# Weight tiles of a float32 decoder block: lower parts by an accumulating DMA, weights three tiles ahead, operands at multiples of 512 bytes

## The chip, the cores and the metric

The kernel runs on one core of a Trainium2 chip, in one launch. The metric is the device time of that launch in microseconds (us); lower is better. The time before is the median of three runs.

## The reference

One decoder block on 512 tokens of width 1024, in float32. Two token mixers work in parallel on x:

```
proj = x @ w_in                       # 1024 x 7168: c_val c_gate q f i g gates
A: c = c_val * sigmoid(c_gate); causal depthwise conv (31); LayerNorm; silu;  y_conv = c @ w_conv_out
B: 8 heads of a gated linear recurrence, head size 128, chunkwise; RMSNorm; * silu(g); y_hgrn = o @ w_hgrn_out
mix = (sigmoid(gate_A)*y_conv + sigmoid(gate_B)*y_hgrn) @ w_out
x = LayerNorm(alpha*x + mix)
u, gv = split(x @ w_ffn_in)           # 1024 x 5632
x = LayerNorm(alpha*x + (gelu(dwconv3(u)) * gv) @ w_ffn_out)     # 2816 x 1024
```

## The kernel before, in words

**Products.** Every large product is made in float32 accuracy from operands in the type fp32r. An operand is a pair (hi, lo): hi is the value rounded to fp32r and lo = value - hi. `mm3` (L152) issues three matmuls, hi*hi, hi*lo and lo*hi, on L154, L155 and L156, into one sum. The first of a group's operands is the one loaded into the array (stationary, 128 columns), the second is streamed (moving, 512 columns, or 256 in the seven-product stages).

**Weight stream.** The weights lie in DRAM as 142 tiles of 128x1024 float32 (512 KB), in the order of their use. `weight(i)` (L139) calls `fetch` for every tile up to i + AHEAD, with AHEAD = 2. `fetch` (L113) loads the raw tile from SyncE's queue (L119; three raw buffers), ScalarE copies it to hi (L135), and VectorE subtracts, lo = raw - hi (L136). hi and lo have rings of four buffers each; eight tiles go to other storage (`resident`). The first eight tiles, of the convolution's input projection, begin the kernel. 88 tiles go through `fetch`; the other 54 are the gates' 16 and 38 of the FFN's, which `weight_sums` (L560) loads, combines and splits for a scheme of seven products of half-size blocks in the place of eight (`seven`, L591); these use the same rings (`ring_pair`, L549).

**Order of the work.** Convolution inputs (tiles 0 to 7, until about 51 us), values and eight heads (`values`, `head`; tiles 8 to 39, until about 289 us), in which the steps of the recurrence are put in between the matmuls of the next projection (`pump`, L268) and the taps of the depthwise convolution run on VectorE in the background (L251); convolution output and half of the recurrence's output (40 to 47); gates in the seven-product scheme (48 to 63, 343 to 420 us); the other half of the output (64 to 67); W_out (68 to 75), for two halves of the tokens; FFN up, three pairs of blocks plain (76 to 81) and 19 by seven products (82 to 119, until 714 us); FFN down (120 to 141). Each engine runs its own instructions in order; the order is laid down when the kernel is built, by program order and readiness, and `urgent` (L543) raises a priority. GpSimd has a part of the recurrence's updates (L352, L393, L426) and one DMA (L947).

**Addresses.** A partition's memory is filled in this order: 16,384 bytes reserved for descriptors of GpSimd's DMAs, four constants of 32 bytes, the pool of constants (2,240 bytes), the weight pool, the pool of temporaries (among them many tiles of under 512 bytes), and the pool of activations. So the weight pool begins at 18,752 = 36*512 + 320 and the activations at 107,712 = 210*512 + 192; the temporaries used as operands begin at 64, 192 or 448 past a multiple of 512. All slices that a matmul takes are multiples of 512 bytes long or apart. Of the 1968 three-part matmuls of 512 columns, stationary and moving operand begin a multiple of 256 bytes apart in 472, and 128 bytes off that in 1496; of the 2556 of 256 columns in 572 and 1984 (counted from the addresses of the kernel before).

Of the kernel before, what the change touches and what calls it, by code (L numbers as in the profile page):

```python
# [35 lines left out]
# columns of the packed per-channel parameters  # L36
# [12 lines left out]
# weight stream: tile numbers  # L49
# [5 lines left out]
GATES = (4, 0, 5, 1, 6, 2, 7, 3)  # the order of the gates' pairs of blocks  # L55
# [9 lines left out]
def hybrid_block(ctx: ExitStack, tc: tile.TileContext, wts: bass.AP, xT_d: bass.AP,  # L65
# [27 lines left out]
    AHEAD = 2  # L93
# [7 lines left out]
    # the activation table and the tensor engine's clock are up before the first data  # L101
    wrm = tmp.tile([P, 512], BF16, tag="mv", name="wrm", bufs=1)
    wrs = const.tile([P, 8], F32, name="wrs")
    ve.memset(wrm, 0.0)
    ve.memset(wrs, 0.0)
    ac.activation(wrs, wrs, AF.Exp)
# [6 lines left out]
    def fetch(i):  # L113
        raw = wp.tile([P, 1024], F32, tag="raw", name=f"wr{i}", bufs=3)
        parts = 4 if i == 0 else 1
        n = 1024 // parts
        pieces = [slice(j * n, j * n + n) for j in range(parts)]
        for c in pieces:
            nc.sync.dma_start(raw[:, c], wts[i][:, c])  # L119
        if i in resident:  # L120
            hi, lo = resident[i]()
        else:
            hi = wp.tile([P, 1024], F32R, tag="hi", name=f"wh{i}", bufs=4)
            lo = wp.tile([P, 1024], F32R, tag="lo", name=f"wl{i}", bufs=4)
        if isinstance(hi, list):
            for j in range(2):
                c = slice(j * 512, j * 512 + 512)
                ac.copy(hi[j], raw[:, c])
                ve.tensor_tensor(lo[j], raw[:, c], hi[j], ALU.subtract)
        else:  # L130
            for c in pieces:
                if parts > 1:
                    ve.tensor_copy(hi[:, c], raw[:, c])
                else:
                    ac.copy(hi[:, c], raw[:, c])  # L135
                ve.tensor_tensor(lo[:, c], raw[:, c], hi[:, c], ALU.subtract)  # L136
        loaded[i] = (hi, lo)
# [14 lines left out]
    def mm3(ps, a, b, start, stop, more=False):  # L152
        """ps += a^T b in float32 accuracy, each operand as (hi, lo); more: onto a sum already read"""
        pe.matmul(ps, a[0], b[0], start=start, stop=False, skip_group_check=more)  # L154
        pe.matmul(ps, a[0], b[1], start=False, stop=False, skip_group_check=more)  # L155
        pe.matmul(ps, a[1], b[0], start=False, stop=stop, skip_group_check=more)  # L156

    def rsqrt(dst, src, n, mult, eps, key):
        """dst = 1/sqrt(src*mult + eps) on [P, n]: a third-order step and Newton's from the guess by the exponent.
        With v = KAPPA*(src*mult + eps), the last step's -27/1024 becomes the result's scale."""  # L160
        v = tmp.tile([P, n], F32, tag=f"rs_x{n}", name=f"rsx_{key}")
        y = tmp.tile([P, n], F32, tag=f"rs_y{n}", name=f"rsy_{key}")
        t = tmp.tile([P, n], F32, tag=f"rs_t{n}", name=f"rst_{key}")
# [10 lines left out]
        q = tmp.tile([P, n], F32, tag=f"rs_q{n}", name=f"rsq_{key}")  # L174
# [13 lines left out]
    p1 = tc.tile_pool(name="p1", bufs=1)  # L188
    p1p = p1.__enter__()
# [8 lines left out]
    cws = [p1p.tile([P, 1054], F32, tag=f"sc{j}", name=f"cws{j}") for j in range(4)]  # L198
# [23 lines left out]
    # lower bounds: softmax over the two rows of logits  # L222
# [3 lines left out]
    mx = tmp.tile([P, HEADS], F32, tag="s_mx", name="mx", bufs=1)  # L226
    e0 = tmp.tile([P, HEADS], F32, tag="s_e0", name="e0", bufs=1)
    e1 = tmp.tile([P, HEADS], F32, tag="s_e1", name="e1", bufs=1)
# [74 lines left out]
    cst = tmp.tile([P, NT, 6], F32, tag="cst", name="cst", bufs=1)  # L303
    cmv = tmp.tile([P, NT, 2], F32, tag="cmv", name="cmv", bufs=1)
    crs = tmp.tile([P, NT], F32, tag="crs", name="crs", bufs=1)
# [31 lines left out]
    def head(h):  # L337
# [7 lines left out]
        # the factor 1-lb of k rides on q  # L345
# [14 lines left out]
        def block_scores(n, cols_of):  # L360
            """psum [s, blk, n] = kt[:, s] . moving columns of the 32-block of s"""
# [8 lines left out]
        def take(ps, c0, hh, i):  # L370
            """scores of t in the odd blocks of hh, where the mask i is set"""
# [23 lines left out]
        def next_tot(hh):  # L395
            nonlocal tot
            tv, n = pairs_of(tot, hh)
            nt = tmp.tile([P, n], F32, tag=f"tot{hh}", name=f"tt{h}_{hh}", bufs=1 if hh < 4 else 2)
            ve.tensor_tensor(nt, tv[:, :, 0], tv[:, :, 1], ALU.mult)  # L399
            tot = nt  # L400
# [9 lines left out]
        def moving(hh):  # L410
            """queries of the levels hh and 2 hh for keys that decay to the end of their block of hh:
            t in the odd blocks of hh; t in the odd blocks of 2 hh, for s in the second half of the even one; the same
            over the whole second half, for s in the first"""
# [9 lines left out]
            # what the keys of a block of 4 hh decay by to its end  # L423
            dk = tmp.tile([P, nr * 16, 3], F32, tag="dk", name=f"dk{h}_{hh}", bufs=1)
# [9 lines left out]
        def s_first():  # L434
            # the diagonal, and pairs
# [54 lines left out]
        def s_state():  # L490
            # states before the blocks 1 to 3
# [10 lines left out]
        def s_out():  # L502
# [6 lines left out]
            ms = tmp.tile([P, NT], F32, tag="ms", name=f"ms{h}")  # L509
            rs = tmp.tile([P, NT], F32, tag="rs", name=f"rs{h}")  # L510
# [30 lines left out]
    # Winograd's form of Strassen's: activations = [[A11, A12], [A21, A22]] by tokens and inputs,  # L541
    # two blocks of 128 outputs = [[B11, B12], [B21, B22]] by inputs and block.
# [6 lines left out]
    def ring_pair(key, extra):  # L549
        """hi and lo of [P, 1024]: the weight stream's slots and, if there is one, a fifth"""  # L550
        out = []
        for tag, more in zip(("hi", "lo"), extra or (None, None)):
            if more is not None and ring_n[0] % 5 == 4:
                out.append(p1p.tile([P, 1024], F32R, tag=more, name=f"s{tag}_{key}"))
            else:
                out.append(wp.tile([P, 1024], F32R, tag=tag, name=f"s{tag}_{key}", bufs=4))
# [3 lines left out]
    def weight_sums(i, t, b21, extra):  # L560
        """the seven weight operands of the stream's tiles i and i+1"""
# [29 lines left out]
    def seven(ring, slots, w, A, S, pc, ug, last):  # L591
        """two blocks of outputs, features by tokens, into ug; last(X) takes the second half of the first"""
# [22 lines left out]
        # a sum is read between two additions to it; with a fifth slot the reads get more time  # L615
# [55 lines left out]
    class Two:  # L671
        """blocks of 256 tokens in two tiles, indexed [:, k]"""
# [60 lines left out]
    # the gated sums, as (hi, lo)  # L733
# [4 lines left out]
    def mixed(m, srcs):  # L738
        """blocks m and m+1"""
# [37 lines left out]
    # W_out stays on chip for both halves of the tokens  # L777
# [24 lines left out]
    def ln1_transposes(half, tb, n):  # L802
# [4 lines left out]
        # gain and shift go by partitions here  # L807
# [7 lines left out]
    def factor_sums(i, sh, sl):  # L815
        """S1..S4 of the activations for the seven-product scheme, 128 tokens of each half"""
# [41 lines left out]
    def hid():  # L858
        """the hidden activations, by blocks of 128 channels, in what is free by now"""
# [35 lines left out]
    def seven_up(j, w, sh, sl):  # L895
        """a pair of blocks of the hidden layer"""
# [62 lines left out]
    def hidden(k):  # L959
        """hidden block k as (hi, lo)"""  # L960
# [39 lines left out]
    for tb in range(NT):  # L1000
# [88 lines left out]
```

## Time and profile before

| | us |
|---|---|
| median of 3 runs | 847.4 |
| lowest and highest | 846.91, 847.9 |
| profiled execution, first to last instruction (span) | 846.1 |

The profile is of one execution; its span leaves out what the run takes before the first and after the last instruction. That execution's own time is not known beside its span, so the median less the span, 1.3 us, stands for what lies around it. Busy shares in the span: TensorE 98%, its weight loads 85%, VectorE 79%, ScalarE 49%, GpSimd 7%. In rows of the trace PE is TensorE's matmul, PEld its weight load, DVE VectorE, ACT ScalarE, POOL GpSimd, SP SyncE. The end of a matmul is modelled, so the spacing of starts says more of TensorE's rate than the duration of one. L-numbers are lines of the kernel before.

### The profile page before, as it was taken

The numbers are of one execution on the slowest core, as the hardware profiler recorded it, in microseconds if no ns is written. First come the engines' busy times: TensorE is split into PE (matmuls) and PEld (weight loads), VectorE is DVE, ScalarE is ACT, GpSimd is POOL, SyncE is SP. The second block draws the span as 40 slices with busy tenths as digits, with TensorE's granted clock in tenths as the row PEclk, the third lists the DMA queues.
The fourth block names the chain that finished last, engine by engine and source line by source line (L and its number), as shares of the span: only waits on it lengthen the run. The fifth ranks groups of instructions, "written<-read, shape, count | busy, mean of one in ns | idle before, by whom it ended". The sixth has DMA issues, their size and how long they took to land.

```text
span 846.1 us, 14434 instructions
## 1 busy us (share of the span) xinstructions
PE 829.9 (98%) x5771; PEld 720.1 (85%) x5771; DVE 666.9 (79%) x1141; ACT 411.8 (49%) x760; POOL 59.0 (7%) x93
## 2 busy tenths in 40 slices
PE   9999999999999999999999999999999999999995
PEld 6888777777777778999988899999999999888884
DVE  5379999999788849688774789699999999753366
ACT  4233443445566755466542646466666666423200
POOL 0000321233211210000000000000000000000000
PEclk9999999999999999999999999999999999999998
DMA  8323212122211224233255331122333224633202
GB/s 291 119 100 100 75 58 92 50 77 76 75 53 51 86 76 157 85 118 105 88 178 207 125 125 53 73 101 100 110 119 122 101 100 139 261 123 105 95 26 75
DMA packets 26659, 90.33 MB, mean 107 GB/s; under 512 B 2912, under 2 KB 3808, under 8 KB 26464
## 3 DMA queue, kind: packets, MB, share of 16 engines
q1 hardware_dynamic: 24288, 82.85, 29.2%
q10 hardware_dynamic: 2160, 4.47, 1.5%
q0 software_dynamic: 144, 2.10, 0.6%
q8 instruction: 45, 0.74, 0.4%
q14 instruction: 22, 0.18, 0.1%
HBM read 85.21 MB, written 4.19 MB: 106 GB/s over the span
## 4 chain that ended last, share of the span: by engine, by line
PE 79%; DVE 16%; ACT 3%; issue 1%; DMA 1%; POOL 0%; DVEq 0%; ACTq 0%; POOLq 0%
PE ps L154 25%; PE ps L156 25%; PE ps L155 25%; DVE cws L251 7%; DVE wl L136 2%; DMA xr<-in_xT 1%; DVE tt L399 1%; PE ps L366 1%; PE ps L521 1%; DVE qq L388 1%; DVE gg L355 1%; ACT wh L135 1%; ACT sq L513 0%; PE ps L506 0%; PE ps L805 0%
## 5 line engine op out<-in xcount | busy, mean ns | idle before, releaser
L136 DVE TENSOR_TENSOR wl<-wr,wh 128x1024 fp32r<-128x1024 f32 (+1 forms) x82 | 100.9, 1233 | 55.1 <-ACT wh L135 55.0
L135 ACT CAST wh<-wr 128x1024 fp32r<-128x1024 f32 x78 | 81.9, 1050 | 126.2 <-PE ps L156 68.2
L154 PE MATMUL ps<-xh,wh 128*128 128x512 f32 x256 | 105.7, 414 | 0.6 <-ACT xh L147 0.6
L155 PE MATMUL ps<-xl,wh 128*128 128x512 f32 x256 | 102.4, 400 | 0.2 <-DVE xl L150 0.2
L156 PE MATMUL ps<-xh,wl 128*128 128x512 f32 x256 | 102.0, 398 | 0.0
L251 DVE SCALAR_TENSOR_TENSOR cws<-cws,par 128x512 f32<-128x512 f32 x120 | 89.2, 772 | 0.0
L154 PE MATMUL ps<-sh,shi_t 128*128 128x256 f32 x228 | 64.3, 282 | 0.0
L156 PE MATMUL ps<-sh,slo_t 128*128 128x256 f32 x228 | 64.3, 282 | 0.0
L155 PE MATMUL ps<-sl,shi_t 128*128 128x256 f32 x228 | 64.2, 282 | 0.0
L154 PEld LDWEIGHTS ps<-xh,wh 128*128 128x128 f32 x256 | 48.6, 190 | 12.1 <-ACT xh L147 2.0
L156 PEld LDWEIGHTS ps<-xh,wl 128*128 128x128 f32 x256 | 48.5, 189 | 10.7
L155 PEld LDWEIGHTS ps<-xl,wh 128*128 128x128 f32 x256 | 48.6, 190 | 10.1 <-DVE xl L150 0.8
L150 DVE TENSOR_TENSOR slo_t<-Toh,shi_t 128x1024 fp32r<-128x1024 f32 x38 | 46.4, 1220 | 11.5 <-ACT shi_t L147 11.4
L147 ACT CAST shi_t<-Toh 128x1024 fp32r<-128x1024 f32 x38 | 39.5, 1041 | 15.9 <-PE ps L155 15.9
L156 PEld LDWEIGHTS ps<-sh,slo_t 128*128 128x128 f32 x228 | 43.1, 189 | 0.0
L154 PEld LDWEIGHTS ps<-sh,shi_t 128*128 128x128 f32 x228 | 43.1, 189 | 0.0
L155 PEld LDWEIGHTS ps<-sl,shi_t 128*128 128x128 f32 x228 | 43.1, 189 | 0.0
L150 DVE TENSOR_TENSOR slo_b<-wr,shi_b 128x1024 fp32r<-128x1024 f32 x27 | 33.0, 1221 | 8.3 <-ACT shi_b L147 8.3
L545 ACT COPY pc<-ps 128x256 f32<-128x256 f32 x57 | 21.1, 370 | 37.0 <-PE ps L156 37.0
L147 ACT CAST shi_b<-wr 128x1024 fp32r<-128x1024 f32 x27 | 28.4, 1050 | 9.2 <-PE ps L155 5.7
L947 POOL DMA_DIRECT2D lnp<-in_ln x1 | 0.7, 717 | 413.5 <-PE ps L156 413.5
L156 PE MATMUL ps<-wh,ht 128*128 128x512 f32 x72 | 28.6, 397 | 0.0
(375 smaller groups left out, 2485.6 us busy)
## 6 DMA issues: line engine op xcount, KB each, us to landing
wr<-in_wts SPq DMA_DIRECT2D x141, 512.0 KB, 3.5
xr<-in_xT ACTq DMA_DIRECT2D x8, 256.0 KB, 4.0
x<-in_x ACTq DMA_DIRECT2D x4, 512.0 KB, 7.3
x_d<-x SPq DMA_DIRECT2D x4, 512.0 KB, 3.5
x1a<-x_d SPq DMA_DIRECT2D x1, 2048.0 KB, 8.5
lnp<-in_ln POOLq DMA_DIRECT2D x1, 2048.0 KB, 11.7
out<-x1a SPq DMA_DIRECT2D x8, 256.0 KB, 2.0
xsqq<-in_xT SPq DMA_DIRECT2D x4, 256.0 KB, 2.7
```

What stands on the lines that cost most here:

```text
L135: ac.copy(hi[:, c], raw[:, c])
L136: ve.tensor_tensor(lo[:, c], raw[:, c], hi[:, c], ALU.subtract)
L147: ac.copy(hi, src)
L150: (lo_eng or ve).tensor_tensor(lo, src, hi, ALU.subtract)
L154: pe.matmul(ps, a[0], b[0], start=start, stop=False, skip_group_check=more)
L155: pe.matmul(ps, a[0], b[1], start=False, stop=False, skip_group_check=more)
L156: pe.matmul(ps, a[1], b[0], start=False, stop=stop, skip_group_check=more)
L251: ve.scalar_tensor_tensor(cacc[j], cpad[j][:, i:i + T], w, cacc[j], ALU.mult, ALU.add)
L355: ve.scalar_tensor_tensor(gg, gg, pcol(PC_NG + h), pg, ALU.mult, ALU.mult)
L366: pe.matmul(ps[32 * j:32 * j + 32, blk], kt[:, b32 * 32:b32 * 32 + 32], cols_of(b32), start=True, stop=True, tile_position=(0, 32 * j))
L388: ve.tensor_tensor(qo, qo, tv[:, :, 0:1].broadcast_to([P, n, hh]), ALU.mult)
L545: f(*args)
```

## The change

In `fetch`, tiles from 8 on: ScalarE copies raw to hi, ScalarE then writes lo = -hi, and a DMA issued by GpSimd adds raw onto lo, in place of VectorE's subtraction. AHEAD goes from 2 to 3 and the rings of hi and lo from four buffers to five (the raw ring keeps three). All small temporaries move to a pool `sml` behind the activations; the descriptors' reserve goes from 16,384 to 4,096 bytes; the warm-up tile `wrs` is padded from 8 to 56 elements and `cws` from 1054 to 1152, so that weight pool, temporaries and activations begin at multiples of 512 bytes and all tiles in them are multiples of 512 long. Comments are dropped.

```diff
-    AHEAD = 2
+    AHEAD = 3
-    wrs = const.tile([P, 8], F32, name="wrs")
+    wrs = const.tile([P, 56], F32, name="wrs")
-    ac.activation(wrs, wrs, AF.Exp)
+    ac.activation(wrs[:, 0:8], wrs[:, 0:8], AF.Exp)
...
-            hi = wp.tile([P, 1024], F32R, tag="hi", name=f"wh{i}", bufs=4)
-            lo = wp.tile([P, 1024], F32R, tag="lo", name=f"wl{i}", bufs=4)
-        if isinstance(hi, list):
+            hi = wp.tile([P, 1024], F32R, tag="hi", name=f"wh{i}", bufs=5)
+            lo = wp.tile([P, 1024], F32R, tag="lo", name=f"wl{i}", bufs=5)
+        if i >= 8:
+            for j in range(2 if isinstance(hi, list) else 1):
+                c = slice(j * 512, j * 512 + 512) if isinstance(hi, list) else slice(0, 1024)
+                h, l = (hi[j], lo[j]) if isinstance(hi, list) else (hi, lo)
+                ac.copy(h, raw[:, c])
+                ac.mul(l, h, -1.0)
+                po.dma_start(l, raw[:, c], accum_op=ALU.add)
+        elif isinstance(hi, list):
...
-    p1 = tc.tile_pool(name="p1", bufs=1)
-    p1p = p1.__enter__()
+    p1p = ctx.enter_context(tc.tile_pool(name="p1", bufs=1))
+    sml = ctx.enter_context(tc.tile_pool(name="sml", bufs=2))
...
-    cws = [p1p.tile([P, 1054], F32, tag=f"sc{j}", name=f"cws{j}") for j in range(4)]
+    cws = [p1p.tile([P, 1152], F32, tag=f"sc{j}", name=f"cws{j}") for j in range(4)]
...
-                out.append(wp.tile([P, 1024], F32R, tag=tag, name=f"s{tag}_{key}", bufs=4))
+                out.append(wp.tile([P, 1024], F32R, tag=tag, name=f"s{tag}_{key}", bufs=5))
...
-            nt = tmp.tile([P, n], F32, tag=f"tot{hh}", name=f"tt{h}_{hh}", bufs=1 if hh < 4 else 2)
+            nt = sml.tile([P, n], F32, tag=f"tot{hh}", name=f"tt{h}_{hh}", bufs=1 if hh < 4 else 2)
...
-    nc = bacc.Bacc("TRN2", target_bir_lowering=False, num_devices=1)
+    nc = bacc.Bacc("TRN2", target_bir_lowering=False, num_devices=1, dynamic_dma_scratch_size=4096)
```

The line with `nt` stands for all that move from `tmp` to `sml`: the tiles of `rsqrt`, s_mx, s_e0, s_e1, cst, cmv, crs, tot2 to tot64, dk, ms, rs, lst, lmv and lrs.

## Rows read from the trace of the kernel before

**Rows 1.** The page: busy us (share of the span) and instructions of each engine.
```profile
PE 829.9 (98%) x5771; PEld 720.1 (85%) x5771; DVE 666.9 (79%) x1141; ACT 411.8 (49%) x760; POOL 59.0 (7%) x93
```

**Rows 2.** Windows: stretch, its length, busy us (starts) of each engine, clock, DMA.
```profile
100.00:150.00 50.00, 49.07 (x387) 38.13 (x386) 49.48 (x102) 21.33 (x57) 10.47 (x15) 1.00 0.23 75
600.00:650.00 50.00, 50.00 (x423) 50.00 (x422) 46.54 (x61) 30.94 (x50) 0.00 (x0) 1.00 0.31 107
100.00:350.00 250.00, 245.29 (x1977) 192.03 (x1976) 213.95 (x493) 133.27 (x325) 50.54 (x75) 1.00 0.24 79
```

**Rows 3.** TensorE in order of time, FFN down, operands a multiple of 256 apart.
```profile
754.27 0.39 PE L154 MATMUL ps<-wh,hq 128*128 128x512 f32 x1
...
756.99 0.39 PE L154 MATMUL ps<-wh,hq 128*128 128x512 f32 x1
```

**Rows 4.** The same view, convolution inputs, operands 128 off.
```profile
26.65 0.40 PE L156 MATMUL ps<-xh,wl 128*128 128x512 f32 x1
...
28.28 0.41 PE L154 MATMUL ps<-xh,wh 128*128 128x512 f32 x1
```

**Rows 5.** The same view, FFN up plain, 256 columns, a multiple of 256 apart.
```profile
505.83 0.28 PE L155 MATMUL ps<-x1l,fir 128*128 128x256 f32 x1
...
507.50 0.28 PE L154 MATMUL ps<-x1h,fir 128*128 128x256 f32 x1
```

**Rows 6.** Line L805, float32 transposes of 128 columns: four in order of time, and one's duration.
```profile
476.19 0.60 PE L805 MATMUL ps<-ident,x 128*128 128x128 f32 x4
...
L805 PE MATMUL ps<-ident,x x8: 270/272/273, 474.4 to 476.5; 128*128 128x128 f32 x8
```

**Rows 7.** The page's groups: busy, mean ns of one, idle before them.
```profile
L136 DVE TENSOR_TENSOR wl<-wr,wh 128x1024 fp32r<-128x1024 f32 (+1 forms) x82 | 100.9, 1233 | 55.1 <-ACT wh L135 55.0
L135 ACT CAST wh<-wr 128x1024 fp32r<-128x1024 f32 x78 | 81.9, 1050 | 126.2 <-PE ps L156 68.2
```

**Rows 8.** TensorE in order of time, a head: a wait for VectorE.
```profile
169.42 0.40 PE L156 MATMUL ps<-xh,wl 128*128 128x512 f32 x1
170.53 0.55 PE L366 MATMUL ps<-mv,kt 128*32 128x48 f32 x32 [0.71 <-DVE mv L422]
```

**Rows 9.** The page: DMA issues, KB each, median us to landing.
```profile
wr<-in_wts SPq DMA_DIRECT2D x141, 512.0 KB, 3.5
x1a<-x_d SPq DMA_DIRECT2D x1, 2048.0 KB, 8.5
lnp<-in_ln POOLq DMA_DIRECT2D x1, 2048.0 KB, 11.7
```

**Rows 10.** Line L947: GpSimd's one DMA, its issue in ns.
```profile
L947 POOL DMA_DIRECT2D lnp<-in_ln x1: 717/717/717, 718.9 to 718.9; - x1
```

**Rows 11.** Tile 64 after the gates: ScalarE's copy, TensorE's first use of lo.
```profile
415.69 1.05 ACT L135 CAST wh<-wr 128x1024 fp32r<-128x1024 f32 x1 [0.94 <-PE ps L155]
420.34 0.40 PE L156 MATMUL ps<-oh,wl 128*128 128x512 f32 x1
```

**Rows 12.** Tile 120 at the start of FFN down, the same.
```profile
704.57 1.05 ACT L135 CAST wh<-wr 128x1024 fp32r<-128x1024 f32 x1
714.55 0.39 PE L155 MATMUL ps<-wl,hkT 128*128 128x512 f32 x1
```

**Rows 13.** Tile 141, the last: the copy of 140, and the first use of 141's lo.
```profile
798.42 1.05 ACT L135 CAST wh<-wr 128x1024 fp32r<-128x1024 f32 x1 [3.98 <-PE ps L156]
807.35 0.40 PE L155 MATMUL ps<-wl,hq 128*128 128x512 f32 x1
```

**Rows 14.** Tile 125, FFN down: VectorE's lower part, TensorE's first use of it.
```profile
735.11 1.22 DVE L136 TENSOR_TENSOR wl<-wr,wh 128x1024 fp32r<-128x1024 f32 x1
743.51 0.39 PE L155 MATMUL ps<-wl,hq 128*128 128x512 f32 x1
```

**Rows 15.** Who waited for whom: us in total, times, longest.
```profile
ACT wh L135 <- PE ps L155: 46.9, 23, 4.5
POOL kt L393 <- PE ps L366: 29.9, 8, 5.6
```

More of the change, by code (lines that the diff above doesn't have):

```diff
@@ L158, in rsqrt @@
     def rsqrt(dst, src, n, mult, eps, key):
-        v = tmp.tile([P, n], F32, tag=f"rs_x{n}", name=f"rsx_{key}")
-        y = tmp.tile([P, n], F32, tag=f"rs_y{n}", name=f"rsy_{key}")
-        t = tmp.tile([P, n], F32, tag=f"rs_t{n}", name=f"rst_{key}")
+        v = sml.tile([P, n], F32, tag=f"rs_x{n}", name=f"rsx_{key}")
+        y = sml.tile([P, n], F32, tag=f"rs_y{n}", name=f"rsy_{key}")
+        t = sml.tile([P, n], F32, tag=f"rs_t{n}", name=f"rst_{key}")
         def vyy():
@@ L173, in rsqrt @@
         vyy()
-        q = tmp.tile([P, n], F32, tag=f"rs_q{n}", name=f"rsq_{key}")
+        q = sml.tile([P, n], F32, tag=f"rs_q{n}", name=f"rsq_{key}")
         ve.scalar_tensor_tensor(q, t, -10.0 / 3.0, t, ALU.add, ALU.mult)
@@ L225, in hybrid_block @@
     lg0, lg1 = pcol(PC_LG, 8), pcol(PC_LG + 8, 8)
-    mx = tmp.tile([P, HEADS], F32, tag="s_mx", name="mx", bufs=1)
-    e0 = tmp.tile([P, HEADS], F32, tag="s_e0", name="e0", bufs=1)
-    e1 = tmp.tile([P, HEADS], F32, tag="s_e1", name="e1", bufs=1)
+    mx = sml.tile([P, HEADS], F32, tag="s_mx", name="mx", bufs=1)
+    e0 = sml.tile([P, HEADS], F32, tag="s_e0", name="e0", bufs=1)
+    e1 = sml.tile([P, HEADS], F32, tag="s_e1", name="e1", bufs=1)
     ve.tensor_tensor(mx, lg0, lg1, ALU.max)
@@ L300, in values @@
             ac.copy(v[tb][:, half * 512:half * 512 + 512], ps[tb])
-    cst = tmp.tile([P, NT, 6], F32, tag="cst", name="cst", bufs=1)
-    cmv = tmp.tile([P, NT, 2], F32, tag="cmv", name="cmv", bufs=1)
-    crs = tmp.tile([P, NT], F32, tag="crs", name="crs", bufs=1)
+    cst = sml.tile([P, NT, 6], F32, tag="cst", name="cst", bufs=1)
+    cmv = sml.tile([P, NT, 2], F32, tag="cmv", name="cmv", bufs=1)
+    crs = sml.tile([P, NT], F32, tag="crs", name="crs", bufs=1)
     cn = [c[:, 0:512] for c in cws]
@@ L422, in moving @@
             ve.tensor_tensor(col(2, 2 * hh), odd(2 * hh), t4.broadcast_to([P, 16, nr, 2 * hh]), ALU.mult)
-            dk = tmp.tile([P, nr * 16, 3], F32, tag="dk", name=f"dk{h}_{hh}", bufs=1)
+            dk = sml.tile([P, nr * 16, 3], F32, tag="dk", name=f"dk{h}_{hh}", bufs=1)
             tv = tot[:, 0:T // hh].rearrange("p (r w) -> p r w", w=4)
@@ L508, in s_out @@
                     pe.matmul(po_[:, ts], qt[:, ts], st[:, tb - 1], start=False, stop=True)
-            ms = tmp.tile([P, NT], F32, tag="ms", name=f"ms{h}")
-            rs = tmp.tile([P, NT], F32, tag="rs", name=f"rs{h}")
+            ms = sml.tile([P, NT], F32, tag="ms", name=f"ms{h}")
+            rs = sml.tile([P, NT], F32, tag="rs", name=f"rs{h}")
             sq = tmp.tile([P, T], F32, tag="t1", name=f"sq{h}")
@@ L760, in normalize @@
     def normalize(r, key):
-        st = tmp.tile([P, 2, 6], F32, tag="lst", name=f"lst{key}")
-        mv = tmp.tile([P, 2], F32, tag="lmv", name=f"lmv{key}")
-        rs = tmp.tile([P, 1], F32, tag="lrs", name=f"lrs{key}")
+        st = sml.tile([P, 2, 6], F32, tag="lst", name=f"lst{key}")
+        mv = sml.tile([P, 2], F32, tag="lmv", name=f"lmv{key}")
+        rs = sml.tile([P, 1], F32, tag="lrs", name=f"lrs{key}")
         for n in range(2):
@@ L1003, in hybrid_block @@
                 down(k, ws[k - NK], tb, (n,))
-        st = tmp.tile([P, 2, 6], F32, tag="lst", name=f"lstb{tb}")
-        mv = tmp.tile([P, 2], F32, tag="lmv", name=f"lmvb{tb}")
-        rs = tmp.tile([P, 1], F32, tag="lrs", name=f"lrsb{tb}")
+        st = sml.tile([P, 2, 6], F32, tag="lst", name=f"lstb{tb}")
+        mv = sml.tile([P, 2], F32, tag="lmv", name=f"lmvb{tb}")
+        rs = sml.tile([P, 1], F32, tag="lrs", name=f"lrsb{tb}")
         halves = [slice(n * 512, n * 512 + 512) for n in range(2)]
@@ L1016, in hybrid_block @@
             nc.sync.dma_start(out[tb * P:tb * P + P, c], x1a[:, tb, c])
-    p1.__exit__(None, None, None)
 def pack(inp):
```

## The prediction

> **What bounds the kernel now.** I read the page first. TensorE is busy 98% of the span, VectorE 79% [rows 1]. The windows by 50 us say which stretch is what: in the early heads VectorE is busy 49.48 of 50 us beside a TensorE at 49.07; in FFN up TensorE never stops and VectorE has 46.54; the clock granted is 1.00 in all of them [rows 2]. So TensorE's own rate sets nearly the whole time, and VectorE stands close behind it in two stages. A busy TensorE says nothing of its rate, so third I read starts in order of time. In FFN down, where the two operands' addresses are a multiple of 256 bytes apart, 12 spacings take 2.72 us, 227 ns each [rows 3]. In the convolution inputs, 128 bytes off that, seven take 1.63 us, 233 ns [rows 4]. For 256 columns the order is turned: 14 spacings of 1.67 us, 119.3 ns, at a multiple of 256 [rows 5], against 50/423 = 118.2 in FFN up, where most are 128 off [rows 2]. The step from 256 to 512 columns costs 226.7 - 119.3 = 107.4 ns, 0.42 ns a column; so each matmul pays some 12 ns beyond its columns, and up to 6 more by where its operands lie.
>
> **The change, part by part.**
>
> *VectorE's subtractions go.* 80 of the 88 tiles leave VectorE, at 1.23 us each [rows 7]: 98 us of work, and most of the 55 us for which it stood before them, waiting for ScalarE's copies. None of this is on TensorE's path in the FFN's seven-product stage, which does not use `fetch`. In FFN down VectorE has time. It pays in the heads, where TensorE is idle 4.7 of 250 us [rows 2] and now and then waits for VectorE. The modelled ends hide a part of such a wait: in one place TensorE shows 0.71 us of idle, but its starts are 1.11 apart where 0.23 is usual, 0.88 too long [rows 8]. 4.7 x 0.88/0.71 is 5.8 us. Bounds of the gain: nothing and 5.8; I take 4, since ScalarE and GpSimd are next behind VectorE.
>
> *ScalarE gets a second pass.* 80 times 1.05 us [rows 7], 84 us on an engine at 49%. Between 100 and 350 us it has 133 of 250 us [rows 2], 53%, and some 30 more passes make 66%. I cost it at nothing; the cover is that idle time. If a pass stands before a copy that a head's output waits for, a head loses up to 1.05 us, 8 in all.
>
> *GpSimd gets the DMAs.* The trace has one DMA from its queue, issued in 717 ns [rows 10], so 80 make 57 us of issue on an engine at 7%. How long an accumulating DMA of 512 KB takes, no row shows. Bounds: 3.5 us, the plain load of 512 KB, and 11.7 us, 2 MB on GpSimd's queue [rows 9]. 2 MB took 8.5 us from SyncE's queue, so GpSimd's adds 3.2; 3.5 + 3.2 = 6.7 us is what I take. From ScalarE's copy to a finished lo it is then 1.05 + 1.05 + 0.72 + 6.7 = 9.5 us, where it was 1.05 + 1.23 = 2.3.
> The Trainium skill ("DMA: Bandwidth & Descriptors", Anatomy of one DMA) gives 2.0 us plus the bytes at 436 GB/s; with raw and lo both read, 1 MB, that is an estimate of 4.4 us. No row shows an accumulation; by that the sum below would be 1 us less.
>
> *Three tiles ahead, five buffers.* Tile i+3 then goes into the buffers of tile i-2, which are free when `weight(i)` is called, as tile i+2 does now; so ScalarE's wait for a free buffer stays what it is, and there is one more tile of lead, 24 matmuls, 5.5 us, to pay the 7.2 us that the path grows by. In the heads and FFN down lo is long finished when it is first used; the shortest lead there is tile 125's, finished at 736.33, used at 743.51, 7.2 us [rows 14]. So nothing is late there. Tight are three places. Tile 64, after the gates: copied at 415.69, needed at 420.34 [rows 11]; with 9.5 us it comes at 425.2, 4.9 late; but with a fifth buffer its place in the ring is free four products of 12 matmuls, 5.7 us, sooner, and then nothing is late. Tile 120: 704.57 + 9.5 = 714.1 against 714.55 [rows 12], in time. Tile 141: its buffer comes free when that of 140 does now, 798.42, and 807.9 is 0.6 after the need at 807.35 [rows 13]. In W_OUT a tile lasts only 12 matmuls, 2.8 us, while three raw buffers at 3.5 + 9.5 us each turn make 4.3 us a tile; what is loaded ahead about covers it. Together I take +2 us. At 3.5 us a DMA it is 0. At 11.7 it is 9.9 for tile 64 (nothing gained by the buffer), 4.6 for 120 and 5.6 for 141: 20.
>
> *Operands at multiples of 512.* Then all pairs are a multiple of 256 apart. What rows show of that state: 1496 matmuls of 512 columns go from 233 to 226.7 ns, -9.3 us; 1984 of 256 columns from 118.2 to 119.3, +2.2 us; together -7. No operand lies at a multiple of 512 now, so the trace can't show whether the 12 ns that each matmul pays go too. Bounds: +2 us (only the second term) and -61 us, when all 12 ns go (472 x 11.9 + 1496 x 18.1 + 572 x 11.9 + 1984 x 10.8 ns). I take -7, the value of the nearest rows.
> The moves to `sml`, the paddings and the smaller reserve issue nothing: 0.
>
> **Sum.** 846.1 - 4 + 2 - 7 = 837 us for the profiled execution's span, and 1.3 around it: 838 us. The span was 846.1 and the median 847.4, so the forecast is 9 us, 1.1%, under the median.
>
> **The rivals.**
>
> *The 12 ns go as well.* For it: the four float32 transposes, with a weight load before each as well, stand (600 - 270)/3 = 110 ns apart, 600 ns being the four and 270 one of them [rows 6], and if a float32 column takes twice 0.42 ns, 128 take 107.4 and the extra is under 3 ns; so a fixed price of changing the weights is not the cause, and the extra depends on addresses in part, as [rows 3, 4] show. Against it: at 233 and 118 ns the extra changes with the distance of the operands, so it can be two streams meeting, which an equal start need not end. With 2.6 ns left, the spacings become 217.4 and 110.0: 472 x 9.3 + 1496 x 15.5 + 572 x 9.3 + 1984 x 8.2 ns = 49 us. In FFN up TensorE then needs 423 x 0.110 = 46.5 us for what VectorE needs 46.54 for, so VectorE gives back some 4. 846.1 - 49 + 4 - 4 + 2 + 1.3 = 800 us; with the bounds of the extra 788 to 815.
> The Trainium skill ("TensorE: Matmul & The Clock Gate", Back-to-back issue gap) has a spacing of columns over 2.4 GHz plus 2.5 ns whatever the address, 215.8 and 109.2 ns. The trace [rows 3 to 5] doesn't agree: 227 to 233 and 119. By it, as an estimate, the alignment would be worth 55 us.
>
> *GpSimd's queue holds the recurrence; slower than before.* Each accumulating DMA waits in GpSimd's order for ScalarE's second pass, and the updates on L393 stand behind it, for which the next step's matmuls wait. For it: ScalarE's copies wait for a free buffer 23 times, up to 4.5 us [rows 15]. Against it: GpSimd stands ready 29.9 us in all before its inputs [rows 15]. A hold is two passes and an issue, 2.8 us; it decides once it outlasts the one to five turns of three matmuls (0.7 us each) between two steps. With one tile of the three per head in that place, 8 x 2.8 = 22 us: 860 us.
>
> *GpSimd can't issue while VectorE works; slower.* Where VectorE is busy 49.48 of 50 us, each issue could wait for one of its instructions, 1.23 us; with 12 tiles in four heads 15 us, 853 us. For it no row; the one issue in the trace took 0.7 us.
> The Trainium skill ("SBUF — State Buffer", SBUF: two separate sides) warns of it: descriptors from GpSimd starve while VectorE holds the shared port in a fast mode. No run here shows it.
>
> *Nothing moves.* VectorE's work was hidden, and the distance of the operands only went along with the stage: 846 to 849 us.
>
> **How the numbers follow.** Chances: forecast 0.45 (its own range 832 to 845); 12 ns go 0.31; GpSimd's queue 0.13; its port 0.03; nothing 0.08. The range 788 to 850 leaves out the two slower rivals and a little below, 0.19. A measurement of this kernel tells about 0.2% from no change. Faster by more: nearly all of 0.45 and 0.31, 0.75; within it 0.10; slower 0.15.
>
> **What the profile after would show.** VectorE near 570 us busy, ScalarE near 495, 80 DMAs on GpSimd's queue landing within 6.7 us or so. In the convolution inputs, which have no accumulating DMA, spacings of 226.7 ns for the forecast, 217 or less for the first rival; in FFN up 119 to 120 or 110, and with 110 VectorE without pauses. A gap before the first use of lo of tiles 64, 120 or 141 tells of a slow DMA; waits of TensorE for L393 of GpSimd's queue. The prediction is wrong if spacings leave 226.7 on either side, or if DMAs land after 12 us.

## The result and the profile after

The changed kernel takes 877.4 us (876.6 to 878.8) against 847.7 for the kernel before beside it: ratio 1.0353, 95% interval 1.034 to 1.0366, so 30 us slower, where 838 was forecast. The profiled span is 876.2 us, 30.1 over the one before. Below, L130 is ScalarE's copy to hi, L131 its second pass, L132 the accumulating DMA, L119 the raw load, L162 to L164 the three matmuls.

The page's busy times, which answer to [rows 1]:

```profile
PE 835.1 (95%) x5771; PEld 726.2 (83%) x5771; DVE 572.5 (65%) x1060; ACT 490.2 (56%) x841; POOL 125.3 (14%) x174
```

The work moved as it was meant to: VectorE has 94 us less, ScalarE 78 more, GpSimd 66 more. TensorE, though, is busy for 5 us more in a span 30 us longer. Windows, as in [rows 2]: two of the same stretches, then W_OUT and the end of FFN down, which had no pauses before.

```profile
600.00:650.00 50.00, 50.00 (x419) 50.00 (x419) 46.05 (x60) 31.53 (x50) 0.00 (x0) 1.00 0.32 106
100.00:350.00 250.00, 245.51 (x1992) 196.28 (x1992) 175.52 (x446) 161.72 (x356) 68.98 (x99) 1.00 0.56 140
...
440.00:445.00 5.00, 5.00 (x24) 4.14 (x23) 0.18 (x1) 2.95 (x4) 1.21 (x2) 1.00 1.06 255
...
450.00:455.00 5.00, 0.00 (x0) 0.00 (x0) 0.00 (x0) 0.00 (x0) 0.00 (x0) 0.63 1.03 328
455.00:460.00 5.00, 4.47 (x12) 3.23 (x12) 0.00 (x0) 4.49 (x5) 1.72 (x2) 0.68 0.62 171
...
820.00:830.00 10.00, 3.02 (x7) 1.32 (x6) 0.69 (x1) 3.60 (x5) 1.72 (x2) 0.67 0.94 199
830.00:840.00 10.00, 5.85 (x13) 4.17 (x14) 1.38 (x2) 1.02 (x1) 0.86 (x1) 0.50 0.27 54
```

The last three columns are the granted clock, the share of the DMA engines and GB/s. From 450 to 455 us no engine computes at all, and the DMA engines are full (1.03). In the stretches with these pauses the granted clock is down: 0.63 and 0.68 in W_OUT, 0.67 and 0.50 at the end; 0.50 is the lower of TensorE's two levels (1.2 of 2.4 GHz). The kernel before, in the 50 us that hold most of W_OUT and in FFN down:

```profile
450.00:500.00 50.00, 50.00 (x267) 42.64 (x266) 30.31 (x66) 18.86 (x36) 0.00 (x0) 1.00 0.41 136
750.00:800.00 50.00, 50.00 (x220) 41.18 (x219) 19.58 (x21) 16.01 (x20) 0.00 (x0) 1.00 0.35 106
```

What TensorE waited for in the whole execution, longest sums first (us, times, longest):

```profile
PE ps L163 <- DMA wl<-wr: 12.5, 6, 4.2
PE ps L163 <- DMA wo_qq<-wr: 6.4, 1, 6.4
PE ps L530 <- ACT on L525: 3.2, 7, 0.8
PE ps L163 <- DMA wo_sc<-wr: 2.6, 1, 2.6
```

L163 is the matmul that first takes lo: hi is there, lo is not. One such pause, in W_OUT (start, duration, and in brackets the idle time before it):

```profile
448.24 0.39 PE L162 MATMUL ps<-wo_qq,mh 128*128 128x512 f32 x1
455.01 0.79 PE L163 MATMUL ps<-wo_qq,mh 128*128 128x512 f32 x1 [6.38 <-DMA wo_qq<-wr]
455.60 0.63 PE L164 MATMUL ps<-wo_qq,mlcl 128*128 128x512 f32 x1
456.03 0.63 PE L162 MATMUL ps<-wo_qq,mh 128*128 128x512 f32 x1
```

The next spacings are 0.43 us instead of 0.227. There are 22 such in W_OUT and at the end, 22 x 0.2 = 4.4 us on top of the pauses. DMA queues (packets, MB, share of the sixteen engines), and issues (KB, median us to landing), as in [rows 9]:

```profile
q1 hardware_dynamic: 24288, 82.85, 28.7%
q0 software_dynamic: 11808, 44.05, 25.6%
...
wr<-in_wts SPq DMA_DIRECT2D x141, 512.0 KB, 4.1
wl<-wr POOLq DMA_DIRECT2D x71, 512.0 KB, 5.3
...
x<-in_x ACTq DMA_DIRECT2D x4, 512.0 KB, 9.2
...
x1a<-x_d SPq DMA_DIRECT2D x1, 2048.0 KB, 18.8
lnp<-in_ln POOLq DMA_DIRECT2D x1, 2048.0 KB, 16.2
...
wo_qq<-wr POOLq DMA_DIRECT2D x1, 512.0 KB, 11.2
```

GpSimd's queue q0 has 25.6% of 876.2 us; 5.1 of these 224 us are `lnp` (0.6% of 843.7 where it is alone there, in the first experiment), so an accumulated tile takes 2.74 us of all sixteen engines (80 tiles); a raw load takes 251/158 = 1.59 (28.7% of the span; 82.85 MB are 158 times 512 KB). Two bursts of other loads lie in these stretches: the four of x, 2 MB, issued from 442.17 to 443.63 us and landed by 456.01, beside which the accumulation of `wo_qq` took 11.2 us; and at the start of FFN down x1a and lnp, 4 MB, from 727.90 to 748.88 us, beside which an accumulation issued at 737.2 took 15.4. The kernel before has the same loads, and no pause. Where the raw loads waited, by SyncE's queue:

```profile
SPq L119 <- DMA wl<-wr: 373.3, 64, 11.4
```

A raw load waits until the accumulating DMA of three tiles earlier has landed and so frees the buffer. The chain of waits at the end of FFN down shows the turn:

```profile
794.91 0.28 issue
795.19 5.98 DMA wl<-wr
801.22 4.62 DMA wr<-in_wts
805.87 1.06 ACT fores L130
...
808.35 6.38 DMA wr<-in_wts
814.76 1.06 ACT wh L130
815.84 0.96 ACT wl L131
816.81 3.49 DMA wr<-in_wts
...
822.84 5.97 DMA wr<-in_wts
828.88 2.41 issue
831.32 4.44 DMA wl<-wr
835.80 0.79 PE ps L163
```

Tile after tile: load, two passes, issue, accumulation, and only then the load of the buffer's next tile. The load issued at 801.22 and the one of 816.81 share a buffer: a turn of 15.6 us, 5.2 a tile over three buffers. From 781.00 to 822.84 there are nine loads, also 5.2 us apart; in W_OUT the eight loads, from 417.49 to 455.02, are 5.4 us apart, where they are 3.0 in the kernel before. TensorE uses a tile in 5.5 us in FFN down, so no lead is gained there, and the last six, wanted within 8.9 us, come at the loads' pace; the last raw load is issued at 822.84, in the kernel before by 790.4.

By stage, worked out from the start of the first matmul on each weight tile in the profiled execution: us before, then the difference to it of each kernel (the experiments follow).

| tiles | before | after | e1 | e2 | e7 | f3 | e9 | e8 | f4 |
|---|---|---|---|---|---|---|---|---|---|
| 0-12 convolution, values | 73.7 | -2.5 | -1.5 | -1.7 | -2.2 | -0.1 | -1.8 | -1.9 | -1.6 |
| 12-40 heads | 215.6 | -3.9 | -0.2 | -3.7 | -3.9 | -3.9 | -4.0 | -3.9 | -3.7 |
| 40-68 to W_OUT | 154.3 | 0.0 | -0.4 | 0.1 | 0.0 | -0.7 | -0.9 | -0.1 | 0.0 |
| 68-76 W_OUT | 46.3 | 11.8 | -0.7 | -0.7 | 0.4 | 8.0 | 7.2 | 4.4 | -0.7 |
| 76-79 FFN up begins | 9.5 | 4.6 | 0.0 | 0.0 | 0.0 | 0.5 | 0.6 | 0.0 | 0.0 |
| 79-120 FFN up | 214.9 | 2.8 | 2.0 | 2.0 | 2.1 | 3.4 | 3.4 | 2.0 | -0.4 |
| 120-135 FFN down | 83.9 | 2.1 | -0.8 | -0.8 | 2.5 | 0.7 | -0.7 | -0.8 | -0.8 |
| 135-141 | 8.9 | 10.4 | -0.1 | -0.1 | 0.9 | 0.4 | -0.1 | -0.1 | -0.1 |
| 141-end | 39.0 | 5.0 | -0.7 | -0.6 | -0.1 | 1.6 | -0.2 | -0.6 | -0.6 |

### The profile page after: what moved, and what is told of

It reads as the page before. It is cut to its first block, busy times and chain, and to the rows that moved or that the text cites. A ratio compares the mean times of both kernels' runs of the same rounds, so it can differ in the third digit from the quotient of the medians.

```text
span 876.2 us, 14633 instructions
## 1 busy us (share of the span) xinstructions
PE 835.1 (95%) x5771; PEld 726.2 (83%) x5771; DVE 572.5 (65%) x1060; ACT 490.2 (56%) x841; POOL 125.3 (14%) x174
## 3 DMA queue, kind: packets, MB, share of 16 engines
q1 hardware_dynamic: 24288, 82.85, 28.7%
q0 software_dynamic: 11808, 44.05, 25.6%
## 4 chain that ended last, share of the span: by engine, by line
PE 56%; DMA 18%; DVE 16%; issue 5%; ACT 5%; POOL 0%; DVEq 0%; ACTq 0%; POOLq 0%; SPq 0%
PE ps L162 17%; PE ps L163 17%; PE ps L164 17%; DMA wr<-in_wts 9%; DVE cws L260 7%; DMA wl<-wr 6%; ACT wl L131 1%; DMA xr<-in_xT 1%; PE ps L375 1%; DMA x_d<-x 1%; DVE qq L397 1%; PE ps L530 1%; ACT sq L522 1%; ACT wh L130 1%; DVE tt L408 1%
## 5 line engine op out<-in xcount | busy, mean ns | idle before, releaser
L132 POOL DMA_DIRECT2D wl<-wr x71 | 62.3, 878 | 555.2 <-ACT wl L131 291.7
L130 ACT CAST wh<-wr 128x1024 fp32r<-128x1024 f32 x71 | 74.5, 1050 | 118.3 <-DMA wr<-in_wts 68.2
L162 PE MATMUL ps<-xh,wh 128*128 128x512 f32 x256 | 105.3, 413 | 0.3 <-ACT xh L155 0.3
L163 PE MATMUL ps<-xl,wh 128*128 128x512 f32 x256 | 100.9, 394 | 0.5 <-DVE xl L158 0.5
L164 PE MATMUL ps<-xh,wl 128*128 128x512 f32 x256 | 100.9, 394 | 0.0
L260 DVE SCALAR_TENSOR_TENSOR cws<-cws,par 128x512 f32<-128x512 f32 x120 | 86.0, 763 | 0.2
L131 ACT ACTIVATE wl<-wh 128x1024 fp32r<-128x1024 f32 x71 | 75.1, 1058 | 0.8
L162 PE MATMUL ps<-sh,shi_t 128*128 128x256 f32 x228 | 64.5, 283 | 0.0
L163 PE MATMUL ps<-sl,shi_t 128*128 128x256 f32 x228 | 64.5, 283 | 0.0
L164 PE MATMUL ps<-sh,slo_t 128*128 128x256 f32 x228 | 64.5, 283 | 0.0
L162 PEld LDWEIGHTS ps<-xh,wh 128*128 128x128 f32 x256 | 48.1, 188 | 11.3 <-ACT xh L155 1.3
L164 PEld LDWEIGHTS ps<-xh,wl 128*128 128x128 f32 x256 | 48.3, 189 | 10.2
L163 PEld LDWEIGHTS ps<-xl,wh 128*128 128x128 f32 x256 | 48.4, 189 | 9.2 <-DVE xl L158 1.3
L162 PEld LDWEIGHTS ps<-sh,shi_t 128*128 128x128 f32 x228 | 43.8, 192 | 0.0
L163 PEld LDWEIGHTS ps<-sl,shi_t 128*128 128x128 f32 x228 | 43.8, 192 | 0.0
L164 PEld LDWEIGHTS ps<-sh,slo_t 128*128 128x128 f32 x228 | 43.8, 192 | 0.0
L163 PE MATMUL ps<-wl,hkT 128*128 128x512 f32 x72 | 28.6, 397 | 5.3 <-DMA wl<-wr 5.3
```

The costliest lines, as they stand in the source:

```text
L130: ac.copy(h, raw[:, c])
L131: ac.mul(l, h, -1.0)
L132: po.dma_start(l, raw[:, c], accum_op=ALU.add)
L260: ve.scalar_tensor_tensor(cacc[j], cpad[j][:, i:i + T], w, cacc[j], ALU.mult, ALU.add)
```

## The experiments

**e1: VectorE's subtraction back.**

```diff
-        if i >= 8:
+        if i < 0:
```

> The changed kernel with VectorE's subtraction put back for all tiles; three tiles ahead, five buffers and the operands at multiples of 512 stay. Theory (the loss is the accumulating DMA's alone: a raw buffer is held until the DMA has landed, and three raw buffers then turn too slowly where tiles are wanted fast): the alignment's -7 us of the prediction is left, 840 us (836 to 843), 512-column spacings at 226.7 ns, no wait of TensorE for weights in W_OUT or at the end. Rival (the longer lead or the new places of operands cost by themselves): over 847 us, and W_OUT or the last six tiles still stall.

Measured: 845.3 us, ratio 0.9967 (0.9955 to 0.998). No pause in W_OUT or at the end, so the loss comes with the accumulating DMA and its path (ScalarE's second pass and GpSimd's issue go with it here). But the operands' places give 2.7 us, not 7.

**e2 and e3: accumulating DMA in the heads only, and from tile 64 on only.**

```diff
-        if i >= 8:
+        if 8 <= i < 64:      # e2
+        if i >= 64:          # e3
```

> Accumulating DMA only for tiles 8 to 63 (values and heads), VectorE's subtraction from tile 64 on. Theory: what the accumulating DMA gains, it gains in the heads, where VectorE is relieved; some 2 to 4 us under the kernel with the subtraction everywhere: 837 us (833 to 840). Rival (relief of VectorE is worth nothing, the 6.5 us that the heads gained are alignment): the same as with the subtraction everywhere within 1 us. Second rival (the DMA's path also costs in the heads): slower than that by 2 us or more.

> Accumulating DMA only from tile 64 on (gates, W_OUT, FFN up plain, FFN down), VectorE's subtraction before. Theory: all of the loss is here: 877 us plus the 2 to 4 that the heads' relief gave, 880 us (876 to 883). Rival (a part of the loss is brought along from the heads, by a late start of the later stages): 870 or less.

Measured: e2 842.4 us, ratio 0.9929 (0.9916 to 0.9941); e3 883.2, 1.0405 (1.0382 to 1.0429). Against e1 the DMA gains 2.9 us in the heads, as expected, and loses 38 behind them; e2's time lies above its range because e1's 845.3 does. The window of the heads, first e1's, then e2's:

```profile
100.00:350.00 250.00, 244.74 (x1991) 193.35 (x1990) 216.51 (x493) 135.51 (x327) 51.00 (x75) 1.00 0.24 77
```

```profile
100.00:350.00 250.00, 245.25 (x2015) 195.76 (x2015) 176.35 (x449) 161.16 (x355) 69.88 (x100) 1.00 0.56 139
```

VectorE goes from 216.5 to 176.4 of 250 us, and 24 more matmuls start in that stretch. The table has the gain in tiles 12 to 40: -0.2 in e1, -3.7 in e2.

**e4: five raw buffers, but four of hi and lo, and two tiles ahead** (the lines for lo, in `ring_pair` and in `weight_sums` are changed likewise).

```diff
-    AHEAD = 3
+    AHEAD = 2
-        raw = wp.tile([P, 1024], F32, tag="raw", name=f"wr{i}", bufs=3)
+        raw = wp.tile([P, 1024], F32, tag="raw", name=f"wr{i}", bufs=5)
-            hi = wp.tile([P, 1024], F32R, tag="hi", name=f"wh{i}", bufs=5)
+            hi = wp.tile([P, 1024], F32R, tag="hi", name=f"wh{i}", bufs=4)
```

> The changed kernel with five raw buffers in the place of three, and four hi and lo buffers and two tiles ahead, as before, in the place of five and three (the same space). Theory (raw buffers held until the DMA has landed): most of the stalls in W_OUT and at the last six tiles go, 850 us (843 to 858). Rival (the DMA engines' own time is the bound: some 2.8 us of all sixteen for an accumulated tile beside 1.6 for its raw load, 4.4 us against 2.8 us of TensorE's work a tile in W_OUT): W_OUT still stalls by 5 us or more and the time is 865 us or more. Second rival (ScalarE's order, a tile's second pass behind the next tile's copy): the stall at the sixth W_OUT tile stays, with the DMA's issue over 5 us behind the copy.

Measured: 868.9 us, ratio 1.0233 (1.0211 to 1.0255), between the theories. The last six tiles lose nothing (-0.1 where the changed kernel lost 10.4), as the held raw buffer has it. W_OUT still loses 11.6, with one pause of 8.0 us, and FFN down up to tile 135 10.4; there TensorE waited for an accumulating DMA that landed after 16.0 us, beside the loads of x1a and lnp. Since the lead was taken away with the space, this run can't say whether the engines' time or the shorter lead did that; f3 and e9 were made for it.

**e6: two tiles ahead, four buffers, VectorE's subtraction.** This is e1 with `AHEAD = 2` and `bufs=4` for hi and lo.

> VectorE's subtraction for all tiles, two tiles ahead and four buffers as in the kernel before; only the operands' places and the pools of the changed kernel stay. With three tiles ahead and five buffers the same took 845.3 us. Theory (the lead is worth nothing while a lower part is finished 2.3 us after the copy begins; what is left is the operands' distance): 845.3 within 1 us. Rival (the longer lead gives a part of the 2.7 us): 847 or more.

Measured: 844.9 us, ratio 0.9965 (0.9951 to 0.9978). The third tile of lead is worth nothing here; the 2.7 us come from the operands' places.

**e7: VectorE for 14 tiles.**

```diff
-        if i >= 8:
+        if 8 <= i < W_OUT or W_OUT + 8 <= i < W_FO + 16:
```

> The changed kernel with VectorE's subtraction for 14 tiles: the eight of W_OUT and the last six of FFN down; the other 66 tiles keep the accumulating DMA. Theory (the loss sits where several tiles are wanted within few matmuls): 845 us (842 to 850), no stall over 1 us in W_OUT and after 800 us. Rival (the loss is spread, since the DMA engines are nearly full in all of FFN down and in the gates): 855 us or more.

Measured: 847.5 us, ratio 0.9997 (0.9988 to 1.0006). 14 of the 80 tiles carry the 30 us by which the changed kernel is slower than the one before. FFN down up to tile 135 still loses 2.5 (one pause of 1.7 us after the start at 734.72), most of the distance to e2.

**e8: a plain copy in the accumulation's place.**

```diff
-                po.dma_start(l, raw[:, c], accum_op=ALU.add)
+                po.dma_start(l, raw[:, c].bitcast(F32R))
```

> The changed kernel with a plain DMA copy of the raw tile in the place of the accumulation, on the same queue, behind the same two passes: the subtraction is left out, the path and its order stay. Theory (the accumulation's own time on the DMA engines, 2.7 us of all sixteen for 512 KB against 1.6 for a plain load, fills them in W_OUT): the DMA share per tile falls to about 1.6 us, W_OUT's stall falls by more than half, 855 us (848 to 862). Rival (the path is long and in order, and raw buffers are held, whatever the DMA does): W_OUT stalls by 7 us or more, 868 us or more.

This kernel leaves out the subtraction. Measured: 843.8 us, ratio 0.9963 (0.9948 to 0.9978), less than either expected. Its DMA rows:

```profile
q0 software_dynamic: 11808, 44.05, 14.2%
...
wl<-wr POOLq DMA_DIRECT2D x71, 512.0 KB, 2.9
```

The same bytes on the same queue behind the same two passes take (0.142 x 845.1 - 5.1)/80 = 1.44 us of the sixteen engines instead of 2.74, and land in 2.9 us instead of 5.3. So passes, issue and order by themselves cost little: the end loses nothing, W_OUT 4.4 us. What costs is that the DMA accumulates, which means reading lo beside raw, and adding. The copy shortens both, though, the hold and the engines' time, so this run can't tell them apart.

**e9: the accumulating DMA reads HBM, not the raw buffer.**

```diff
-                po.dma_start(l, raw[:, c], accum_op=ALU.add)
+                po.dma_start(l, wts[i][:, c], accum_op=ALU.add)
```

> The changed kernel with the accumulating DMA reading the tile from HBM a second time, not from the raw buffer; so a raw buffer is free once ScalarE has copied it, some 1 us after its load, and none is held by the DMA. Theory of the held raw buffer: the stalls of the last six tiles go, and in W_OUT too if the hold is the cause there: 850 us (845 to 858). Theory of the DMA engines' time: the last six gain but W_OUT stalls as before by 8 us or more, and the loads that run ahead may fill the engines elsewhere: 862 to 872 us.

Measured: 851.2 us, ratio 1.0039 (1.0025 to 1.0052). This tells the two apart at the end, and in W_OUT in part:

```profile
q0 software_dynamic: 11808, 44.05, 29.1%
...
wl<-in_wts POOLq DMA_DIRECT2D x71, 512.0 KB, 5.9
```

```profile
SPq L119 <- ACT wh L130: 249.3, 55, 14.1
```

The accumulation takes longer than in the changed kernel (5.9 us) and more of the engines ((0.291 x 849.7 - 5.1)/80 = 3.03 us a tile), yet the kernel is 26 us faster, because raw loads now wait for ScalarE's copy and no longer for the DMA. The last six tiles lose nothing. In W_OUT 7.2 of the 11.8 us stay, although its raw loads are now issued 3.3 us apart: the DMA engines are at 0.99 from 440 to 470 us, and accumulations that hold no raw buffer land there after 16.1 and 19.5 us (the window, and the issues of `wo_ol`):

```profile
440.00:470.00 30.00, 24.64 (x100) 19.15 (x99) 6.34 (x13) 8.62 (x11) 3.45 (x4) 0.94 0.99 274
```

```profile
wo_ol<-in_wts POOLq DMA_DIRECT2D x2, 512.0 KB, 17.8
```

So behind the ring stands the engines' time; how much of it is the burst of x no run shows.

**f2: the second pass of W_OUT's tiles on VectorE.**

```diff
-                ac.mul(l, h, -1.0)
+                if W_OUT <= i < W_OUT + 8:
+                    ve.tensor_scalar(l, h, -1.0, None, ALU.mult)
+                else:
+                    ac.mul(l, h, -1.0)
```

> The changed kernel with the second pass (lo = -hi) of W_OUT's eight tiles on VectorE, which is idle there, in the place of ScalarE; the accumulating DMA stays. In the changed kernel ScalarE's second pass of the sixth W_OUT tile stood 9.3 us behind its copy, since the next tile's copy, which waited for its load, was ahead of it in ScalarE's order. Theory (the raw buffers held by the DMAs are the cause, the order only adds): that tile's stall of 2.7 us goes and some of the slow clock behind it, 873 us (868 to 877). Rival (ScalarE's order is the cause in W_OUT): 865 us or less.

Measured: 876.1 us, ratio 1.0332 (1.031 to 1.0355); not told from the changed kernel, so the rival's 865 us are not met. It does not clear ScalarE's order altogether: tiles 68 to 79 lose 7.4 us and not 16.4, and a new wait of 4.6 us for VectorE, just ahead of W_OUT, took half of that back and may itself have given the weight stream time.

**f3: a fourth raw buffer, and 512 bytes less of the reserve to make room.**

```diff
-        raw = wp.tile([P, 1024], F32, tag="raw", name=f"wr{i}", bufs=3)
+        raw = wp.tile([P, 1024], F32, tag="raw", name=f"wr{i}", bufs=4)
-    nc = bacc.Bacc("TRN2", target_bir_lowering=False, num_devices=1, dynamic_dma_scratch_size=4096)
+    nc = bacc.Bacc("TRN2", target_bir_lowering=False, num_devices=1, dynamic_dma_scratch_size=3584)
```

> The changed kernel with a fourth raw buffer, nothing else of the weight stream changed (three tiles ahead, five hi and lo buffers; the space is found by a reserve smaller by 512 bytes). Theory of the held raw buffer: a turn of load, two passes, issue and DMA of about 14 us is shared by four buffers in the place of three, 3.5 us a tile and not 4.6; over eight tiles of W_OUT 9 us and over the last six 6 us: 862 us (855 to 868). Theory of the DMA engines' time: the same load on them, 870 us or more.

Measured: 858.4 us, ratio 1.0134 (1.0111 to 1.0157): 19 us for 4 KB a partition, the same DMAs on the same engines. What TensorE waits for then:

```profile
PE ps L163 <- DMA wo_ol<-wr: 4.5, 1, 4.5
PE ps L163 <- DMA wl<-wr: 3.1, 3, 1.6
```

The 12.5 us of waits for `wl` are now 3.1, and the last six tiles lose 0.4 instead of 10.4. In W_OUT the raw loads are 4.5 us apart and 8.0 of the 11.8 us stay: the buffer helps there by a third.

**f4: e2, and FFN up's activations 128 bytes on.**

```diff
-    x1h = p1p.tile([P, 2, KD, 256], F32R, tag="xh", name="x1h")
+    def off(tag, name, kb):
+        return p1p.tile([P, kb * 1024 + 128], F32R, tag=tag, name=name)[:, 32:32 + kb * 1024]
+    x1h = off("xh", "x1h", 4).rearrange("p (h k t) -> p h k t", h=2, k=KD)   # x1l, sh, sl likewise
```

> Accumulating DMA for tiles 8 to 63 only (842.4 us), and the activations of FFN up placed 128 bytes behind their buffers' start, so that 1884 of the matmuls of 256 columns have operands 128 off a multiple of 256. Theory (the distance of the operands alone sets the spacing): 119.98 ns become 118.7, 1.28 ns x 1884 = 2.4 us, 840 us (839 to 841). Rival (the distance went along with something else, or VectorE is the bound there): spacings stay at 119.9 or the time stays at 842.4 within 1 us.

Measured: 839.8 us, ratio 0.9907 (0.9892 to 0.9921): as expected, and faster than both kernels. FFN up, 50 us of it:

```profile
600.00:650.00 50.00, 50.00 (x424) 50.00 (x423) 46.53 (x61) 31.74 (x51) 0.00 (x0) 1.00 0.32 106
```

The window counts 424 matmuls where the changed kernel has 419; over all stretches without a pause the spacing is 118.7 ns (1866 spacings) against 119.98 (2516).

**f6: GpSimd subtracts, tiles 8 to 63.**

```diff
+        if 8 <= i < 64:
+            ac.copy(hi, raw)
+            po.tensor_tensor(lo, raw, hi, ALU.subtract)
```

> No accumulating DMA: for tiles 8 to 63 GpSimd computes the subtraction that VectorE did, VectorE does the others. Theory (the heads gain by any relief of VectorE): 842 us, as with the accumulating DMA there, if a subtraction on GpSimd takes under some 5 us. Rival (GpSimd is too slow, or holds the recurrence's updates on its queue, or slows VectorE down): 846 us or more.

Measured: 900.4 us, ratio 1.0617 (1.0602 to 1.0633). The convolution's taps on VectorE, first in e2, then in f6, and GpSimd's subtraction:

```profile
L260 DVE SCALAR_TENSOR_TENSOR cws<-cws,par 128x512 f32<-128x512 f32 x120 | 86.0, 766 | 0.2
```

```profile
L263 DVE SCALAR_TENSOR_TENSOR cws<-cws,par 128x512 f32<-128x512 f32 x120 | 108.3, 949 | 0.1
...
L127 POOL TENSOR_TENSOR wl<-wr,wh 128x1024 fp32r<-128x1024 f32 x40 | 101.5, 2538 | 87.3 <-ACT wh L126 87.3
```

A subtraction takes 2.5 us, well under the bound of the first theory, but a tap takes 949 ns on average instead of 766: the 28 of the 120 that overlap a subtraction take 1.62 us on average and up to 2.89, the other 92 0.75. So subtracting on GpSimd makes VectorE's taps 22 us longer in all; issuing DMAs there didn't (763 ns in the changed kernel). And GpSimd, which stood 87.3 us before its subtractions until ScalarE's copies came, held up the recurrence: TensorE waited once for 13.3 us for an update on it (qq, L364). Tiles 12 to 40, counted as in the table, lose 46.5 us; how these divide between the two is not shown.

The Trainium skill ("SBUF — State Buffer", SBUF: two separate sides) has VectorE and GpSimd share a pair of ports as an exclusive lock, also where VectorE reads two inputs while GpSimd reads from the same memory; the taps beside a subtraction agree, at 1.62 us instead of 0.75. Its warning that descriptors from GpSimd starve is for a mode of VectorE that takes both ports; no run shows whether VectorE was in it, and in the changed kernel no such wait shows: the 71 issues took 863 ns in the median and 1275 at most.

## Why the prediction was wrong

*The step that failed* is "what is loaded ahead about covers it", the +2 us (bounds 0 to 20) for three tiles ahead and five buffers. Its own figure, 4.3 us a tile for three raw buffers against 2.8 us of TensorE in W_OUT, made 12 us over eight tiles, and was set aside. Measured it was 5.4 us a tile there, and W_OUT lost 11.8 us and the start of FFN up 4.6. That 12 and 11.8 agree is luck in part: with a fourth raw buffer 8.0 us of W_OUT's loss stayed (f3), and with no hold 7.2 (e9). The second half of the step looked at the wrong ring: tile 141 was timed by its hi and lo buffers ("its buffer comes free when that of 140 does now", 798.42 [rows 13]), while its raw load waited for three turns of the raw ring and was issued at 822.84. The last six tiles and what follows lost 15.4 us. With 2.1 in FFN down the term is some 34 us and not +2 (some 37 against e1, which has the operands' new places and no loss here). f3 and e9 show the raw ring as the cause of the loss at the end and at the start of FFN up, by one more buffer and by no hold, and of a third or so of W_OUT's; e7 shows the place. The rest of W_OUT's loss came while the DMA engines were full, and fell to 4.4 us with the shorter DMA of e8; that it is the engines' time is likely, but no run shows it alone.

*The accumulating DMA*, 6.7 us to landing (bounds 3.5 to 11.7): 5.3 in the median, 4.4 at least; but up to 11.2 in W_OUT and 15.4 in FFN down, where the DMA engines are full. The size was near in the mean, and the price was paid where the mean doesn't hold. What no term had was the engines' time: 2.74 + 1.59 = 4.3 us a tile is more than the 2.8 us in which W_OUT uses one, even without the 2 MB of x.
The Trainium skill ("Collectives: The Full Stack", Stop ④ — SDMA + CCE) calls the addition in the DMA path free between two reads and a write. e8 doesn't speak against it: the accumulating DMA took 1.9 times as much of the engines as the copy, but it reads lo and raw where the copy reads raw alone, and no run tells the second read from the addition.

*VectorE's subtractions*, -4 us (0 to 5.8): the heads gain 3.5 us more in e2 than in e1, a part of it the shorter spacings that e1 could not use. It was right in size.

*ScalarE's second pass*, 0: right in the heads, which gain with it. In W_OUT it stays open: f2 moved it without a gain in all, but with one inside W_OUT.

*Operands at multiples of 512*, -7 us (+2 to -61): the spacings came as read from [rows 3 to 5], 226.9 ns in the convolution inputs (185 spacings) and 119.98 for 256 columns; the 12 ns that each matmul pays stayed, so the first rival is out. But e1 and e6 gain 2.7 us. FFN up lost its 2.0. (The 118.2 ns read from [rows 2] are a little low: the window's count takes in matmuls that lie across its ends; the 420 that start in it are 118.8 apart.) Of the 1496 matmuls that became faster 672 are in tiles 12 to 40, where VectorE set the pace (216.5 of 250 us busy in e1): there e1 gains 0.2. Saved spacings count only where TensorE is the bound, which the prediction itself had read from [rows 2].
The gap that the first rival quotes from the Trainium skill ("TensorE: Matmul & The Clock Gate", Back-to-back issue gap) is in that section the one of a single matmul by itself, and not of a stream with a weight load before each matmul, as here.

*Tile 64* [rows 11]: not late, as forecast; its first use came 5.9 us earlier than before. *Tile 120* [rows 12]: not late by itself. *GpSimd's queue holding the recurrence*: TensorE waited 0.6 us in all for its updates in the changed kernel. Of the rivals on the slower side, none had the raw ring.

## What to carry to other kernels

A buffer is held as long as its last reader runs: when a fast reader is replaced by a long DMA, work out the turn (load, passes, issue, landing) over the number of *its* buffers, and compare it with the time in which the consumer takes a tile, stage by stage; where the turn is longer, the loss is the difference times the tiles, and where it is equal there is no lead for the next rush. Use the long path only where the relieved engine is the bound (here the heads), and leave the short one where the stream is. Fix the hold before the cost of the DMA: one more buffer was worth 19 us, a source that isn't held 26. Then add up the DMA engines' time of everything that a stage loads: in W_OUT 7 to 8 us were lost even so.

## What the runs showed of the hardware

On the average of 80 tiles an accumulating DMA of 512 KB took 2.74 us of the sixteen DMA engines from on-chip memory and 3.03 from HBM (e9), against 1.44 for the plain copy (e8). Operands at a multiple of 512 are no better than at one of 256: 226.7 ns in FFN down before [rows 3] and after (176 spacings from 760 to 800 us); for 256 columns a distance of 128 bytes off is the faster one, 118.7 against 119.98 ns, worth 2.4 us of FFN up in f4 (2.0 in e2, -0.4 in f4). VectorE's tap of 0.75 us took up to 2.89 us beside a subtraction on GpSimd (f6). After TensorE's pauses of 6.4 and 2.6 us in W_OUT its matmuls started 0.43 us apart instead of 0.227, at a clock of 0.66 to 0.68 in those windows.
